# Exponentials and an index row in PSUM, fewer candidate additions, later weight reductions and a fixed order of the last products, in a decoder block on one core

## The chip, the cores and the metric

The kernel runs on one core of a Trainium2 chip. A core has a matrix engine (TensorE, PE in the profile, with PEld for its weight loads), a vector engine (VectorE, DVE), an activation engine (ScalarE, ACT), a general engine (GpSimd, POOL) and SyncE (SP), whose queue issues most DMAs. Each engine works through its own list of instructions in order and waits on semaphores for the others. Matmul results land in PSUM (8 banks of 128 x 512 fp32 here), everything else lies in SBUF. The metric is the device time of one execution in microseconds.

## What is computed

A decoder block over 512 tokens of 1024 channels: block-sparse attention and an RWKV-7 time mix run side by side, are merged by gates, and a product-key expert layer (PEER) follows. The parts that matter here, cut from the reference:

```python
mod = (jax.nn.silu(c) @ w_ada[l] + b_ada[l])[:, None, :]
sh1, sc1, gt1, sh2, sc2, gt2 = jnp.split(mod, 6, axis=-1)
...
qm = rope_partial(rms_norm(qm.reshape(B, S, MOBA_HEADS, HEAD_DIM), q_norm_g[l]), positions)
km = rope_partial(rms_norm(km.reshape(B, S, MOBA_HEADS, HEAD_DIM), k_norm_g[l]), positions)
...
w = -jax.nn.softplus(-(w0 + jnp.tanh(zw) @ w2)) - 0.5
decay = jnp.exp(-jnp.exp(w.astype(f32)))
...
top_s, top_i = lax.top_k(s, PEER_TOPK)
cand_s = (top_s[:, :, 0, :, None] + top_s[:, :, 1, None, :]).reshape(T, PEER_HEADS, PEER_TOPK * PEER_TOPK)
cand_i = (top_i[:, :, 0, :, None] * PEER_NKEYS + top_i[:, :, 1, None, :]).reshape(T, PEER_HEADS, PEER_TOPK * PEER_TOPK)
best_s, best_j = lax.top_k(cand_s, PEER_TOPK)
idx = jnp.take_along_axis(cand_i, best_j, axis=-1)
```

The expert layer then computes, for 384 of the tokens, gelu(x U) times a gate matrix times V over all 16384 experts in 128 blocks, and for the first 128 tokens it gathers the chosen rows of U and V one by one.

## The kernel before

The program is one list of operations; a scheduler that simulates the engines sets the order on each engine, by the priority of an operation (the order in the text, or a high-priority section), and by pacing hints (`follow`) that put one instruction behind another of the same engine without a wait. All matrix products of fp32 are made as three products of rounded halves (hi and lo).

The stages in order of time, with the lines of the profile:

- To about 98 us: the adaLN vector, the first norm, and the first columns of the input projection.
- 98 to 211 us: `rwkv_in`. For each of four groups of 128 channels (p = 0 to 3) `decays` (L481) makes e2 and e3, the falling and the growing exponentials of the summed decays (both 128 x 516, in SBUF, L494 and L495), and `elementwise` (L509) multiplies with them: KK (POOL, L515), the new kk (L517, L518), Kq (L525), RR (POOL, L527). Results go to DRAM. Meanwhile PE works on the queries and keys (`w_tm`, L452), and `qk_part` (L566) normalises each half of a result: sum of squares (L573), an inverse root by Newton steps (L161 to L166, eleven small DVE operations on 128 x 8), gain and rotation on POOL (L578 to L588), the product (L589) and four transposes on PE (L594).
- `inverses(0)` and `tokens(0)` (L387 on PE) start inside this stage; the inverse of chunk 0 solves its 16 x 16 blocks by thirty dependent small DVE operations (L661, L662; tile Yd).
- 211 to 560 us: the RWKV chunks, at high priority, with the attention (`scores`, `outputs`) and the gate projections (`gates`, `w_cm`, L422) as filling on PE; how much filling stands between two steps of the chain is set by `fill`.
- Through all this, `mods` computes the other four adaLN vectors in 32 steps. One step is a DMA of 512 KB of w_ada (wmod, three buffers, L175) and a multiply with a sum along the row on DVE (L176). Every `w_cm` and every second half of a `w_tm` calls one step.
- 560 to 700 us: projections, merge and second norm; 700 to 805 us: `queries`, which takes the top 16 of each score row on DVE.
- About 806 to 1030 us: `best`, for four tiles of 128 tokens. `best_of` (L1001) sums the candidates (nine additions of scores on DVE and nine of indices on POOL: L1017 eight times, L1019 once), takes the top 16 and finds their expert index: a comparison with the row 0 to 49 (`iota`, in SBUF, L1026), a product (L1027, on DVE for tile 1 and on POOL for the others) and a sum (L1029), 64 times each.
- From 875 us: 96 steps of `gates_dense`, each a one-hot pair (L1221 compares with a copy of `iota` that lies in PSUM, tile `iop`; L1225 on DVE or L1230 and L1231 on ACT) and four matmuls (L1238), with the dense products x U between them (`dense_h`, L1178; POOL or DVE make the lo half, L1172).
- To about 2014 us: `dense_v` and `products` (L1305) for each of 128 blocks; six PSUM accumulators, two for each 128 tokens t. At the end the accumulators are scaled, added and stored (L1335 to L1337).

Of the kernel before, what the change touches and what calls it, by code (L numbers as in the profile page):

```python
# [63 lines left out]
def kernel(ctx: ExitStack, tc: tile.TileContext, A):  # L64
# [501 lines left out]
    def qk_part(ps, hf, qi, g):  # L566
        qf = ahalf("qn")
        qn = qf.rearrange("p (h j) -> p h j", h=8)
        ACT.copy(qf, ps)
        sq = ahalf("qsq").rearrange("p (h j) -> p h j", h=8)  # L570
        ACT.activation(sq, qn, AF.Square)
        ss = sm.tile([128, 8], F32, name="qss")
        DVE.tensor_reduce(ss, sq, axis=AX.X, op=ALU.add)  # L573
# [11 lines left out]
        POOL.tensor_tensor(r1, x[:, :, :, 0:16], table(0, 0), op=ALU.mult)
        for a in (0, 8):
            POOL.tensor_tensor(r2[:, :, :, a:a + 8], x[:, :, :, 8 - a:16 - a], table(1, a), op=ALU.mult)
        POOL.tensor_tensor(x[:, :, :, 0:16], r1, r2, op=ALU.add)  # L588
        DVE.tensor_tensor(qn, qn, bc3(y, 64), op=ALU.mult)  # L589
        pT = attile()  # L590
        for c in range(2):
# [821 lines left out]
```

## Time and profile before

| | |
|---|---|
| median of 3 runs (range) | 2023.93 us (2022.27 to 2029.1) |
| the profiled execution | 2025.54 us |
| its span, first to last instruction | 2023.8 us |
| PE busy | 1915.9 us (95%) |
| DVE busy | 1510.3 us (75%) |
| ACT, POOL busy | 828.3 us, 775.6 us |
| mean granted clock of TensorE | 0.979 |

Busy shares are means over stages with different limits, so the rows below go by stage: windows give busy time of each engine and the granted clock of a stretch, waits say who waited for whom, and the timeline lists instructions with start and duration. An instruction that is held up inside its engine shows as a long duration, not as idle time.

### The profile page before, as it was taken

The numbers are of one execution on the slowest core, as the hardware profiler recorded it, in microseconds if no ns is written. First come the engines' busy times: TensorE is split into PE (matmuls) and PEld (weight loads), VectorE is DVE, ScalarE is ACT, GpSimd is POOL, SyncE is SP. The second block draws the span as 40 slices with busy tenths as digits, with TensorE's granted clock in tenths as the row PEclk, the third lists the DMA queues.
The fourth block names the chain that finished last, engine by engine and source line by source line (L and its number), as shares of the span: only waits on it lengthen the run. The fifth ranks groups of instructions, "written<-read, shape, count | busy, mean of one in ns | idle before, by whom it ended". The sixth has DMA issues, their size and how long they took to land.

```text
span 2023.8 us, 29453 instructions
## 1 busy us (share of the span) xinstructions
PE 1915.9 (95%) x10509; PEld 1669.0 (82%) x10509; DVE 1510.3 (75%) x3268; ACT 828.3 (41%) x1367; POOL 775.6 (38%) x631
## 2 busy tenths in 40 slices
PE   7987899999989899888999999999999999999997
PEld 5666777787868888877899998888899999999985
DVE  7798665546445578999977876888756788888885
ACT  5443233323313433356777763333333333333332
POOL 5555210010105322566656663222212444544551
PEclk9998899999989899999999999999999999999999
DMA  8664233321446423435568989999967999999893
GB/s 288 211 202 134 81 115 98 102 93 49 156 138 195 127 80 97 131 110 165 180 199 278 322 303 388 356 354 346 333 219 245 337 335 351 326 351 331 306 346 131
DMA packets 204326, 450.79 MB, mean 223 GB/s; under 512 B 16649, under 2 KB 105225, under 8 KB 204178
## 3 DMA queue, kind: packets, MB, share of 16 engines
q1 hardware_dynamic: 167024, 314.54, 46.1%
q0 software_dynamic: 36864, 134.23, 18.3%
q8 instruction: 83, 1.36, 0.3%
q14 instruction: 65, 0.53, 0.1%
q10 hardware_dynamic: 290, 0.13, 0.0%
HBM read 393.13 MB, written 55.71 MB: 222 GB/s over the span
## 4 chain that ended last, share of the span: by engine, by line
PE 69%; DVE 17%; DMA 4%; issue 2%; ACT 1%; POOL 0%; POOLq 0%; SPq 0%; DVEq 0%; ACTq 0%
PE acc L1305 23%; PE mm L1178 17%; PE mm L422 10%; PE rwp L387 8%; PE mm L452 4%; DMA vf<-in_peer_v 2%; PE pg L1238 2%; DVE ohg L1225 2%; DVE eq L1026 2%; DVE oh L1221 1%; DVE idf L1029 1%; DVE row L1143 1%; PE atp L868 1%; PE atp L842 1%; PE atp L994 1%
## 5 line engine op out<-in xcount | busy, mean ns | idle before, releaser
L1178 PE MATMUL mm<-x,whi 128*128 128x384 f32 x2048 | 542.2, 345 | 1.7 <-ACT ge L1183 1.7
L1178 PEld LDWEIGHTS mm<-x,whi 128*128 128x128 f32 x2048 | 372.7, 190 | 5.6 <-ACT ge L1183 2.0
L1178 PE MATMUL mm<-x,wlo 128*128 128x384 f32 x1024 | 350.8, 343 | 9.5 <-POOL wlo L1172 9.5
L1171 ACT CAST whi<-wf 128x1024 fp32r<-128x1024 f32 x128 | 134.7, 1052 | 290.8 <-PE mm L1178 223.7
L1305 PE MATMUL acc<-vl,ah 128*128 128x512 f32 x768 | 237.6, 390 | 2.7 <-DVE vl L1296 2.7
L1305 PE MATMUL acc<-vh,al 128*128 128x512 f32 x768 | 237.2, 390 | 0.0
L412 POOL TENSOR_TENSOR wlo<-wf,whi 128x1024 fp32r<-128x1024 f32 x33 | 80.9, 2450 | 399.2 <-ACT whi L409 309.9
L1305 PE MATMUL acc<-vh,ah 128*128 128x512 f32 x768 | 206.7, 390 | 3.3 <-ACT vh L1295 3.2
L1178 PEld LDWEIGHTS mm<-x,wlo 128*128 128x128 f32 x1024 | 194.6, 190 | 11.1 <-POOL wlo L1172 10.9
L1172 POOL TENSOR_TENSOR wlo<-wf,whi 128x1024 fp32r<-128x1024 f32 x66 | 163.5, 2479 | 102.4 <-ACT whi L1171 102.3
L1120 POOL DMA_INDIRECT row<-in_peer_u,gidx x96 | 113.2, 1179 | 233.2 <-DVE gh L1143 223.0
L1120 POOL DMA_INDIRECT row<-in_peer_v,gidx x86 | 124.1, 1443 | 154.1 <-DVE gacc L1150 142.5
L1296 DVE TENSOR_TENSOR vl<-vf,vh 128x1024 fp32r<-128x1024 f32 x128 | 157.5, 1231 | 22.5 <-ACT vh L1295 21.9
L1305 PEld LDWEIGHTS acc<-vh,ah 128*128 128x128 f32 x768 | 143.7, 188 | 34.5 <-ACT vh L1295 5.2
L1305 PEld LDWEIGHTS acc<-vl,ah 128*128 128x128 f32 x768 | 143.6, 188 | 31.0 <-DVE vl L1296 3.5
L1305 PEld LDWEIGHTS acc<-vh,al 128*128 128x128 f32 x768 | 144.1, 188 | 30.0
L1295 ACT CAST vh<-vf 128x1024 fp32r<-128x1024 f32 x128 | 134.7, 1054 | 17.2 <-DMA vf<-in_peer_v 17.2
L422 PE MATMUL mm<-X,whi 128*128 128x512 f32 x400 | 135.7, 411 | 3.3 <-ACT z L472 3.3
L1172 DVE TENSOR_TENSOR wlo<-wf,whi 128x1024 fp32r<-128x1024 f32 x62 | 75.9, 1224 | 84.1 <-ACT whi L1171 83.9
L1238 PE MATMUL pg<-ohg,oh 128*128 128x128 f32 x768 | 117.3, 287 | 22.0 <-ACT ohg L1231 15.2
L1143 DVE CUSTOM_DVE_ANT_0 row<-row,xtok 128x1024 f32<-128x1024 f32 x96 | 131.7, 1380 | 4.4 <-DMA row<-in_peer_u,gidx 4.4
L1238 PEld LDWEIGHTS pg<-ohg,oh 128*128 128x128 f32 x768 | 108.0, 192 | 31.6 <-ACT ohg L1231 19.0
(1195 smaller groups left out, 3807.5 us busy)
## 6 DMA issues: line engine op xcount, KB each, us to landing
wf<-in_peer_ut SPq DMA_DIRECT2D x128, 512.0 KB, 4.9
vf<-in_peer_v SPq DMA_DIRECT2D x128, 512.0 KB, 6.0
wmod<-in_w_ada SPq DMA_DIRECT2D x48, 512.0 KB, 4.3
G_d<-stg SPq DMA_DIRECT2D x12, 2048.0 KB, 9.4
wf<-in_w_in_c SPq DMA_DIRECT2D x30, 512.0 KB, 3.9
ge_d<-ge SPq DMA_DIRECT2D x50, 192.0 KB, 2.5
ger<-ge_d SPq DMA_DIRECT2D x50, 192.0 KB, 6.3
wf<-in_peer_wq SPq DMA_DIRECT2D x16, 512.0 KB, 3.5
```

The costliest lines, as they stand in the source:

```text
L387: i = f(*a, **k)
L422: i = fill(PE.matmul(ps, l[:, ks], r(k), start=k == 0 and n == 0, stop=k == nk - 1 and n == 2), 512)
L452: i = fill(PE.matmul(ps[:, c0:c0 + 256], l(4 * kh + k)[:, ts], r[:, cs], start=kh == 0 and tt % 2 == 0 and k == 0 and n == 0, stop=kh == 1 ...
L1120: i = POOL.indirect_dma_start(out=row, out_offset=None, in_=A[key], in_offset=bass.IndirectOffsetOnAxis(ap=gidx[:, s_:s_ + 1], axis=0))
L1143: DVE.tensor_tensor_reduce(out=row, in0=row, in1=xtok, op0=ALU.mult, op1=ALU.add, scale=1.0, scalar=0.0, accum_out=gh[:, s_:s_ + 1])
L1171: ACT.copy(uh, f)
L1172: (POOL if e < LAG else DVE).tensor_tensor(ul, f, uh.bitcast(F32), op=ALU.subtract)
L1178: i = PE.matmul(ps[:, 0:NTD], l[:, ks], r[:, k, 128:512], start=n == 0, stop=n == 23)
L1238: i = PE.matmul(pg[:, t * 128:(t + 1) * 128], oh2[:, t], ohg[:, t], start=True, stop=True)
L1295: ACT.copy(vh, f)
L1296: DVE.tensor_tensor(vl, f, vh.bitcast(F32), op=ALU.subtract)
L1305: i = PE.matmul(acc[2 * t + d], l[:, ts], r[:, d * 512:(d + 1) * 512], start=e == 0 and l is ah and r is vh, stop=e == 127 and l is al)
```

## The change

Six parts, all in one diff:

1. The growing exponentials e3 are written by ACT to a PSUM bank (`rwtile`) instead of SBUF, without their first column; that column and the last of e2 go to `ee` by two small ACT operations instead of two DVE copies.
2. A second copy of `iota` is put in PSUM (`ioe`) before `queries`, and the comparison of `best_of` reads it there.
3. The candidates are summed in six additions instead of nine: rows of equal length are taken together, with one candidate more (NCAND 51).
4. `qk_part` for one half becomes `qk_parts` for both: one Newton iteration on 128 x 16 in place of two on 128 x 8; the transposes are issued later, in the middle of the next `w_tm`, behind given matmuls (`marks`).
5. The 32 steps of `mods` are called by a variable number: none in `rwkv_in` and for queries and keys, one for the values and the first gates, two from the second gates on.
6. For the last two blocks of `products`, the matmuls of one t follow those of the t before.

```diff
-        mods(1, i)
+        mods(nmod[0], i)
...
             if tt == 3:
-                mods(1, i)
+                mods(nmod[0], i)
+            marks.append(i)
...
-        e2, e3 = half4_("e2"), half4_("e3")
+        e2, e3 = half4_("e2"), v4(rwtile())
         ACT.activation(e2, sg, AF.Exp, scale=-0.5 * KAPPA)
-        ACT.activation(e3, sg, AF.Exp, scale=0.5 * KAPPA)
-        DVE.tensor_copy(ee[:, :, 0, p], e3[:, :, 0])
-        DVE.tensor_copy(ee[:, :, 1, p], e2[:, :, 128])
+        ACT.activation(e3, sg[:, :, 1:], AF.Exp, scale=0.5 * KAPPA)
+        ACT.activation(ee[:, :, 0, p], sg[:, :, 0], AF.Exp, scale=0.5 * KAPPA)
+        ACT.activation(ee[:, :, 1, p], sg[:, :, 128], AF.Exp, scale=-0.5 * KAPPA)
...
-        DVE.scalar_tensor_tensor(v4(kk), v4(kk), 0.5, e3[:, :, 1:], op0=ALU.mult, op1=ALU.mult)
+        DVE.scalar_tensor_tensor(v4(kk), v4(kk), 0.5, e3, op0=ALU.mult, op1=ALU.mult)
...
-        DVE.tensor_tensor(v4(zk), v4(zk), e3[:, :, 1:], op=ALU.mult)
+        DVE.tensor_tensor(v4(zk), v4(zk), e3, op=ALU.mult)
...
+    def qk_parts(pss, qi, g):
+
+        ss, y, t = [sm.tile([128, 2, 8], F32, name=n) for n in ("qss", "qy", "qt")]
...
         newton(ss, y, t)
...
+        def channels_first(after):
+            for hf, qf in enumerate(qfs):
+                pT = attile()
+                for c in range(2):
+                    for i in range(2):
+                        o = (2 * c + i) * 128
+                        m = PE.transpose(pT[:, o:o + 128], qf[:, i * 256 + c * 128:i * 256 + (c + 1) * 128], ident)
+                        follow(m, after[hf])
...
                 pss = w_tm(A["w_in_t"][2 * qi + g], X)
-                for hf in range(2):
-                    qk_part(pss[hf], hf, qi, g)
+                if later:
+                    later.pop()(marks[2:4])
+                later.append(qk_parts(pss, qi, g))
...
-            for r1 in range(8):
-                n = 16 // (r1 + 1)
-                eng.tensor_tensor(dst[:, :, off:off + n], src[:, :, 0, r1:r1 + 1].broadcast_to([128, 4, n]), src[:, :, 1, 0:n], op=ALU.add)
-                off += n
+            for r1, m, n in ((0, 1, 16), (1, 1, 8), (2, 1, 5), (3, 2, 4), (5, 3, 2)):
...
-            DVE.tensor_tensor(eq, bc3(bf_[:, h_, k_:k_ + 8], NCAND), bcm(iota[:, 0:NCAND], 8), op=ALU.is_equal)
+            DVE.tensor_tensor(eq, bc3(bf_[:, h_, k_:k_ + 8], NCAND), bcm(ioe[0][:, 0:NCAND], 8), op=ALU.is_equal)
...
     attend(0)
+    nmod[0] = 2
     gates(range(G0, G1))
...
+    ioe.append(attile())
+    ACT.copy(ioe[0][:, 0:128], iota)
+    queries(first_q)
...
                         i = PE.matmul(acc[2 * t + d], l[:, ts], r[:, d * 512:(d + 1) * 512],
                                       start=e == 0 and l is ah and r is vh, stop=e == 127 and l is al)
+                        if len(es) > 1:
+                            follow(i, last)
```

The order that the scheduler makes of it, at three places. First DVE, in the middle of the thirty dependent steps of chunk 0's block inverse (tiles tm and Yd); L176 is a step of `mods`, qss, qy and qt belong to the norms of queries and keys. Before:

```order
L662 TENSOR_TENSOR Yd<-Yd,tm 128x8x8
L176 ISA wmod,modc<-wmod,scr 128x1024
L176 ISA modc 128x1
L661 TENSOR_TENSOR tm<-R,Yd 128x8x7
L573 TENSOR_REDUCE qss<-qsq 128x8
L662 TENSOR_TENSOR Yd<-Yd,tm 128x8x7
L574 TENSOR_SCALAR qss<-qss 128x8
L661 TENSOR_TENSOR tm<-R,Yd 128x8x6
L161 TENSOR_SCALAR qy<-qss 128x8
L662 TENSOR_TENSOR Yd<-Yd,tm 128x8x6
L162 TENSOR_SCALAR qy<-qy 128x8
```

and the same steps now:

```order
L681 TENSOR_TENSOR Yd<-Yd,tm 128x8x8
L680 TENSOR_TENSOR tm<-R,Yd 128x8x7
L681 TENSOR_TENSOR Yd<-Yd,tm 128x8x7
L680 TENSOR_TENSOR tm<-R,Yd 128x8x6
L681 TENSOR_TENSOR Yd<-Yd,tm 128x8x6
L680 TENSOR_TENSOR tm<-R,Yd 128x8x5
L681 TENSOR_TENSOR Yd<-Yd,tm 128x8x5
L680 TENSOR_TENSOR tm<-R,Yd 128x8x4
L579 TENSOR_REDUCE qss<-qsq 128x8
L681 TENSOR_TENSOR Yd<-Yd,tm 128x8x4
```

The reductions and almost all norm operations have left the chain. Between the first kk of p = 0 and the end of this chain, 9 steps of `mods` stood on DVE before, and none stands there now.

Second DVE, in the chunk steps between 260 and 560 us, where the steps of `mods` now stand (XX and XT are steps of chunk 1's inverse, rc and P belong to the attention's softmax):

```order
L864 ISA mx 128x1
L176 ISA wmod,modc<-wmod,scr 128x1024
L176 ISA modc 128x1
L176 ISA wmod,modc<-wmod,scr 128x1024
L176 ISA modc 128x1
L870 RECIPROCAL rc<-se 128x1
L710 TENSOR_TENSOR XX<-XX,rwp 128x512
L715 TENSOR_TENSOR XT<-XT,rwp 128x512
```

Most of them come in pairs; between the end of chunk 0's block inverse and the end of the last one there are 28 steps of `mods` now, and there were 17.

Third PE, the end of the program. Before, block 127's products of the rounding remainders (vl and al) end with all six accumulators:

```order
L1305 MATMUL acc2_11818<-vl_18381,ah_18374 128x512
L1305 MATMUL acc3_11819<-vl_18381,ah_18374 128x512
L1305 MATMUL acc2_11818<-vh_18380,al_18375 128x512
L1305 MATMUL acc3_11819<-vh_18380,al_18375 128x512
L1305 MATMUL acc4_11820<-vl_18381,ah_18374 128x512
L1305 MATMUL acc5_11821<-vl_18381,ah_18374 128x512
L1305 MATMUL acc4_11820<-vh_18380,al_18375 128x512
L1305 MATMUL acc5_11821<-vh_18380,al_18375 128x512
```

Now (vh_18263 is of block 126, vh_18274 of block 127):

```order
L1335 MATMUL acc3_11713<-vh_18274,al_18269 128x512
L1335 MATMUL acc4_11714<-vh_18263,ah_18257 128x512
L1335 MATMUL acc5_11715<-vh_18263,ah_18257 128x512
L1335 MATMUL acc4_11714<-vl_18264,ah_18257 128x512
L1335 MATMUL acc5_11715<-vl_18264,ah_18257 128x512
L1335 MATMUL acc4_11714<-vh_18263,al_18258 128x512
L1335 MATMUL acc5_11715<-vh_18263,al_18258 128x512
L1335 MATMUL acc4_11714<-vh_18274,ah_18268 128x512
L1335 MATMUL acc5_11715<-vh_18274,ah_18268 128x512
L1335 MATMUL acc4_11714<-vl_18275,ah_18268 128x512
L1335 MATMUL acc5_11715<-vl_18275,ah_18268 128x512
```

The last twelve matmuls all go to the accumulators 4 and 5, so 0 to 3 are complete twelve matmuls before the end.

## Rows read from the trace of the kernel before

**Rows 1.** From the page: busy time of each engine in us, with the share of the span and the count of instructions.

```profile
PE 1915.9 (95%) x10509; PEld 1669.0 (82%) x10509; DVE 1510.3 (75%) x3268; ACT 828.3 (41%) x1367; POOL 775.6 (38%) x631
```

**Rows 2.** Windows: for stretches of the span (start:end, length), busy us and count of PE, PEld, DVE, ACT and POOL, then the granted TensorE clock (1.00 is 2.4 GHz, 0.5 is 1.2 GHz), DMA share, GB/s.

```profile
97.70:154.20 56.50, 50.48 (x246) 36.13 (x247) 50.09 (x78) 23.31 (x36) 29.21 (x26) 0.97 0.64 205
154.20:188.60 34.40, 23.59 (x135) 19.23 (x134) 32.75 (x83) 13.25 (x24) 20.72 (x23) 0.80 0.50 166
188.60:211.30 22.70, 14.47 (x112) 13.19 (x110) 19.65 (x60) 6.38 (x10) 9.01 (x11) 0.90 0.28 85
...
260.00:560.00 300.00, 296.08 (x1890) 234.72 (x1890) 165.38 (x424) 95.62 (x220) 30.02 (x16) 1.00 0.33 104
...
700.00:800.00 100.00, 100.00 (x527) 85.24 (x526) 74.02 (x461) 31.87 (x50) 21.55 (x21) 1.00 0.24 78
800.00:870.00 70.00, 58.89 (x326) 57.21 (x324) 66.02 (x287) 24.57 (x35) 44.15 (x43) 0.95 0.41 128
870.00:1000.00 130.00, 113.51 (x665) 106.95 (x665) 130.00 (x404) 84.92 (x137) 83.78 (x90) 0.96 0.47 146
1000.00:1060.00 60.00, 57.81 (x366) 56.78 (x367) 47.52 (x109) 45.83 (x79) 32.27 (x19) 0.97 0.64 199
...
1300.00:1970.00 670.00, 670.00 (x3276) 597.74 (x3275) 535.91 (x658) 239.65 (x324) 253.50 (x203) 1.00 0.90 322
```

**Rows 3.** Waits of PE over the whole span: what waited for what, us in total, times, longest.

```profile
PE pg L1238 <- ACT ohg L1231: 15.2, 12, 2.8
PE mm L1178 <- POOL wlo L1172: 9.5, 3, 5.5
PE atp L594 <- DVE qn L589: 8.3, 1, 8.3
PE rwp L387 <- DVE Dk L645: 7.5, 3, 4.5
```

**Rows 4.** Timeline of DVE, 855 to 880 us: start us, duration us, engine, line, operation, tiles, shapes. L1026 reads two SBUF operands, L1221 one in SBUF and one in PSUM (atp).

```profile
872.23 2.47 DVE L1026 TENSOR_TENSOR eq<-wa,iota 128x400 f32<-128x400 f32 x1
...
876.50 0.68 DVE L1221 TENSOR_TENSOR oh<-sT,atp 128x512 f32<-128x512 f32 x1
```

**Rows 5.** Timeline of POOL in the same stretch; L1172 reads two SBUF operands.

```profile
871.54 2.73 POOL L1172 TENSOR_TENSOR wlo<-wf,whi 128x1024 fp32r<-128x1024 f32 x1
...
876.40 2.37 POOL L1172 TENSOR_TENSOR wlo<-wf,whi 128x1024 fp32r<-128x1024 f32 x1
```

**Rows 6.** Five lines of DVE, each from the view of that line: count, duration in ns (least/median/most), first and last start. L645 reads SBUF alone, without POOL beside it.

```profile
L1026 DVE TENSOR_TENSOR eq<-wa,iota x64: 522/566/2701, 822.1 to 1027.6; 128x400 f32<-128x400 f32 x64
...
L1221 DVE TENSOR_TENSOR oh<-sT,atp x96: 664/678/690, 874.6 to 1197.7; 128x512 f32<-128x512 f32 x96
...
L518 DVE SCALAR_TENSOR_TENSOR kk<-kk,e x4: 694/1970/2774, 101.8 to 158.0; 128x512 f32<-128x512 f32 x4
...
L525 DVE TENSOR_TENSOR zk<-zk,e x4: 819/1673/2819, 107.7 to 164.5; 128x512 f32<-128x512 f32 x4
...
L645 DVE TENSOR_TENSOR Dk<-C,dl x16: 678/689/698, 173.9 to 486.3; 128x512 f32<-128x512 f32 x16
```

**Rows 7.** The step of `mods` (L176) alone, over the three stretches 97.7 to 211.3 us: DVE busy us.

```profile
sum 113.60, DVE 12.01; mean DVE 4.00
```

**Rows 8.** Groups of instructions by line over the whole span: count, busy us, mean ns, idle before. L165 and L166 are two of the Newton steps of the query and key norms.

```profile
L518 DVE SCALAR_TENSOR_TENSOR kk<-kk,e 128x512 f32<-128x512 f32 x4 | 7.4, 1852 | 0.1
...
L525 DVE TENSOR_TENSOR zk<-zk,e 128x512 f32<-128x512 f32 x4 | 7.0, 1746 | 0.0
...
L165 DVE SCALAR_TENSOR_TENSOR qt<-qt,qss 128x8 f32<-128x8 f32 x24 | 5.1, 211 | 0.3
...
L166 DVE SCALAR_TENSOR_TENSOR qy<-qt,qy 128x8 f32<-128x8 f32 x24 | 5.0, 211 | 0.3
```

**Rows 9.** Timeline of DVE, chunk 0's block inverse: its start, two of its steps and a step of `mods` between them, its end.

```profile
188.62 0.22 DVE L658 COPY Yd<-dl 128x128 f32<-128x128 f32 x1
...
198.15 2.31 DVE L662 TENSOR_TENSOR Yd<-Yd,tm 128x72 f32<-128x72 f32 x1
...
200.90 1.22 DVE L176 CUSTOM_DVE_ANT_0 wmod<-wmod,scr 128x1024 f32<-128x1024 f32 x1
...
210.50 0.17 DVE L662 TENSOR_TENSOR Yd<-Yd,tm 128x8 f32<-128x8 f32 x1
```

**Rows 10.** Groups of DVE by line in 800 to 1060 us.

```profile
L1026 DVE TENSOR_TENSOR eq<-wa,iota 128x400 f32<-128x400 f32 x64 | 54.6, 880 | 0.0
...
L1017 DVE TENSOR_TENSOR wb<-vi 128x8 f32<-128x8 f32 (+5 forms) x56 | 11.8, 267 | 0.0
```

**Rows 11.** Timeline of the end, all engines: block 126's first products on PE, block 127's vl on DVE, the last products, and the scaling and the last addition of the outputs.

```profile
2005.44 1.52 PE L1305 MATMUL acc<-vh,ah 128*128 128x512 f32 x6
...
2006.73 1.23 DVE L1296 TENSOR_TENSOR vl<-vf,vh 128x1024 fp32r<-128x1024 f32 x1 [0.43 <-ACT vh L1295]
...
2011.76 1.29 DVE L1335 TENSOR_TENSOR o<-acc,gt 128x512 f32<-128x512 f32 x2 [3.81 <-PE acc L1305]
...
2013.15 0.61 PE L1305 MATMUL acc<-vh,al 128*128 128x512 f32 x2
...
2018.02 1.26 POOL L1336 TENSOR_TENSOR o<-o,hh 128x512 f32<-128x512 f32 x1 [1.83 <-DVE o L1335]
```

More of the change, by code (lines that the diff above doesn't have):

```diff
@@ L29 @@
 NWF = 3
-NCAND = 50
+NCAND = 51
 LAG = 66
@@ L398 @@
     nsplit = [0]
+    nmod, marks = [0], []
     def wload(src):
@@ L564 @@
     qT, kT, vtok = {}, {}, {}
[L566 to L573, printed above, removed]
+    def qk_parts(pss, qi, g):
+        ss, y, t = [sm.tile([128, 2, 8], F32, name=n) for n in ("qss", "qy", "qt")]
+        qfs = []
+        for hf in range(2):
+            qf = ahalf("qn")
+            ACT.copy(qf, pss[hf])
+            sq = ahalf("qsq").rearrange("p (h j) -> p h j", h=8)
+            ACT.activation(sq, qf.rearrange("p (h j) -> p h j", h=8), AF.Square)
+            DVE.tensor_reduce(ss[:, hf], sq, axis=AX.X, op=ALU.add)
+            qfs.append(qf)
@@ L585, in qk_part @@
[L585 to L591, printed above, removed]
-            for i in range(2):
-                o = (2 * c + i) * 128
-                PE.transpose(pT[:, o:o + 128], qf[:, i * 256 + c * 128:i * 256 + (c + 1) * 128], ident)
@@ L595, in qk_part, with table @@
-        dst = kvhalf("qkT")
-        ACT.copy(dst, pT)
-        for c in range(2):
-            (qT, kT)[qi][hf, 2 * g + c] = v2(dst)[:, c]
+        for hf, qf in enumerate(qfs):
+            qn = qf.rearrange("p (h j) -> p h j", h=8)
+            POOL.tensor_tensor(qn, qn, qkg[:, qi:qi + 1].broadcast_to([128, 8, 64]), op=ALU.mult)
+            r1, r2 = [at.tile([128, 2, 4, 16], F32, name=nm, bufs=1) for nm in ("r1", "r2")]
+            x = qf.rearrange("p (i h j) -> p i h j", i=2, h=4)
+            def table(n, a):
+                return sincos[:, 2 * hf:2 * hf + 2, n:n + 1, a:a + 8 if n else 16].broadcast_to([128, 2, 4, 8 if n else 16])
+            POOL.tensor_tensor(r1, x[:, :, :, 0:16], table(0, 0), op=ALU.mult)
+            for a in (0, 8):
+                POOL.tensor_tensor(r2[:, :, :, a:a + 8], x[:, :, :, 8 - a:16 - a], table(1, a), op=ALU.mult)
+            POOL.tensor_tensor(x[:, :, :, 0:16], r1, r2, op=ALU.add)
+            DVE.tensor_tensor(qn, qn, bc3(y[:, hf], 64), op=ALU.mult)
@@ new lines, in channels_first @@
+        def channels_first(after):
+            for hf, qf in enumerate(qfs):
+                pT = attile()
[4 more added lines that the diff above has]
+                        follow(m, after[hf])
+                dst = kvhalf("qkT")
+                ACT.copy(dst, pT)
+                for c in range(2):
+                    (qT, kT)[qi][hf, 2 * g + c] = v2(dst)[:, c]
@@ L600, in qkv @@
+        return channels_first
     def qkv():
+        later = []
         for qi in (1, 0):
@@ L608, in qkv @@
         for g in range(2):
+            nmod[0] = 1
             pss = w_tm(A["w_in_t"][4 + g], X)
+            if later:
+                later.pop()(marks[2:4])
             for tt in range(4):
@@ L884 @@
     hd_ = [dr.tile([128, 4, 2, 256], F32, name=f"h_d{i}") for i in range(2)]
-    vals, inds = {}, {}
+    vals, inds, ioe = {}, {}, []
     def top16(src, v, ix):
@@ L1299, in products @@
     def products(es, parts):
+        i = None
         for t in range(3):
-            ts = slice(t * 128, (t + 1) * 128)
+            ts, last = slice(t * 128, (t + 1) * 128), i
             for e, (ah, al, vh, vl) in zip(es, parts):
```

17 lines of the change are left out of this document (9 added, 8 removed).

## Prediction

> **What bounds the kernel now.** I read the page first: PE is busy for 95% of the span and DVE for 75% [rows 1]. Then the windows [rows 2], where the two bounds part. From 1300 to 1970 us PE is busy for all 670 us at a clock of 1.00, and from 260 to 560 us for 296 of 300 us: there only PE's own work counts, and the change takes none away. Two stretches are different. From 97.7 to 211.3 us PE is busy for 50.5 + 23.6 + 14.5 = 88.5 of 113.6 us, and its granted clock is 0.97, 0.80 and 0.90; DVE is busy for 50.1 + 32.8 + 19.7 = 102.5 us. From 800 to 1060 us PE is busy for 230.2 of 260 us at 0.95 to 0.97, and DVE for 243.5, without a gap from 870 to 1000 us. The waits of PE [rows 3] name DVE directly (qn, Dk), or ACT and POOL, which in these stretches work on what DVE or the same SBUF operands give them. So DVE sets the pace in both, and what a busy DVE does there must be seen next.
>
> The timeline shows it [rows 4, 5]. The comparison L1026 starts at 872.23 and takes 2.47 us; POOL's L1172 runs from 871.54 to 874.27, and the comparison ends just behind it. L1221, a larger comparison that reads its index row from PSUM, starts at 876.50 inside another L1172 (876.40 to 878.77) and takes 0.68 us. Over all instances [rows 6] L1026 goes from 522 to 2701 ns with a median of 566, L1221 from 664 to 690. So a DVE operation with two SBUF operands stands still while POOL reads SBUF, and one with an operand in PSUM does not. L518 and L525, which read e3 from SBUF, show the same (694 to 2774 and 819 to 2819 ns).
>
> **The change part by part: 97.7 to 211.3 us.**
> Steps of `mods`: nine leave, 12.0 us of DVE [rows 7].
> e3 in PSUM: L518 and L525 take 7.4 + 7.0 = 14.4 us for eight operations [rows 8]; at 0.69 us, the time of L645 and the least of L518 [rows 6], they take 5.5, so 8.9 less.
> Newton steps: one call of eleven operations and a scaling goes for every two. Six of the eight calls stand before the end of chunk 0's inverse, so 3 x 12 = 36 operations of 0.21 us [rows 8] leave, 7.6 us by their durations; as neighbours overlap in DVE's pipeline I count 6.
> The two copies to `ee` I count at nothing: on DVE they are small, and on ACT, busy for 23.3 of 56.5 us in the first of the three windows [rows 2], the small exponentials lie beside other work. If that cover fails, four pairs of them delay the tanh behind them; eight at no more than the 0.69 us of a 512-wide operation would be about 5 us.
> Together 27 us of DVE. How much of it is on the path? The least is the wait of 8.3 us for qn [rows 3]: PE stood before the transposes until the block inverse on DVE was through, and both the transposes (now behind matmuls of the next `w_tm`, with qn finished before the inverse starts) and the chain have been freed. The inverse runs from 188.62 to 210.67, 22 us for thirty small operations, with a step of `mods` of 1.22 us and a stall of 2.31 us among them [rows 9]; most of what stood between them is gone, and the stalls behind POOL stay. The most is all 27 us: PE has 25.1 us idle, and 0.03 x 56.5 + 0.20 x 34.4 + 0.10 x 22.7, doubled, is 21.7 us at 1.2 GHz, in which matmuls take twice as long. PE still has to wait for data that go through DRAM and for ACT, so I take two thirds, 18 us, between the ends 8 and 27.
>
> **800 to 1060 us.**
> The 64 comparisons take 54.6 us [rows 10]; at the median of 566 ns they take 36.2, so 18.4 less. Reading PSUM costs nothing more by L1221 (678 ns for 512 elements) against L645 (689 ns for as many in SBUF) [rows 6].
> [...]
> Additions: 24 fewer on DVE, at no more than L1017's mean of 0.27 us [rows 10] 6.5 us, and at half of that, as they overlap, 3. NCAND 51 adds 2% to 64 comparisons, products and sums, about 2 us by the 566 ns, of which most products lie on POOL; I count 1 on DVE.
> So 20 us less for DVE. PE has 29.8 us idle there and about 2 x (0.05 x 70 + 0.04 x 130 + 0.03 x 60) = 21 us at 1.2 GHz [rows 2], so there is room for it. But products of tile 1 (L1027 on DVE) and the additions still read two SBUF operands and will stand behind POOL where they come next, and PE waits for ACT's one-hot rows too (15.2 us [rows 3]). I take three quarters, 15 us; the ends are 6 and 20.
> The bank that `ioe` takes leaves two instead of three for scores in `queries`. PE is busy for all of 700 to 800 us [rows 2], which hides it: I count nothing. Uncovered it is at most a copy's time for each of 16 score banks, 16 x 0.69 = 11 us by an operation of 512 elements.
>
> **260 to 560 us, and the end.**
> The 32 steps of `mods` move here and behind: 28 instead of 17 between the first and the last block inverse, mostly in pairs, ahead of steps of the chain such as XX, and queued in front of them. Eleven more at 1.22 us [rows 9] are 13.4 us of DVE, which is busy for 165 of 300 us [rows 2], and each chain step has filling on PE beside it. With 17 steps all idle time of PE is 3.9 us; in proportion 28 would make it 6.4. I take 2 us of loss, between -1 (the DMAs of w_ada leave the early stage) and 13. On SP's queue the wmod loads are now in pairs ahead of weights and chunk loads; the DMA share there is 0.33, which hides them.
> The end: before, PE's last product ends at 2013.76 and POOL's last addition at 2019.28, 5.5 us later, because all six accumulators come free together [rows 11]. Now only two outputs are left: two scalings (1.29 us as in the row) and POOL's addition (1.26) end 2.7 us after the last product. The new order makes block 127's vl (ready at 2007.96) needed after 8 of its matmuls, at 2005.44 + 8 x 0.25 = 2007.44 (1.52 us for six, as in the row), so PE waits 0.5 us. The gain is 5.5 - 2.7 - 0.5, about 2 us; the ends are 0 and 3.
>
> The sum: 18 + 15 + 2 - 2 = 33 us. The profiled execution took 2025.54 us for a span of 2023.8, 1.7 us around it, and the median of the runs is 1.6 us below it. So the span becomes about 1991, and from the median 2023.93 - 33, rounded, 1991 us. The bounds together give gains from 8 + 6 + 0 - 13 = 1, to 27 + 20 + 3 + 1 = 51 us.
>
> **Rivals.**
> The stall moves on. POOL runs as before, and the next DVE operation with two SBUF operands (L517, L521, the additions, L1027) waits where e3 or L1026 waited. For it speaks that L1026, L1027 and L1017 come in a row; against it, that after 870 us L1027 is POOL's own and most of DVE's neighbours of L1026 are L1221, L1225 and L1029, which read at most one operand from SBUF. Then half of 8.9 and of 18.4 is left, 13.7 less, and with the shares on the path the gain is about 33 - 10, and if PE's chains through ACT also hold, 15: 2009 us.
> PE gains its clock as well. If the gaps close, the 21.7 + 21 us at 1.2 GHz shrink too, PE does its work sooner, and the whole bound is reached: 51 us, near 1975. Against it: DVE then is still as long as PE in both stretches.
> The time does not change: the DVE time falls away but PE waits for ACT and DRAM in the same places, and the early gain is lost before 560 us. For it speaks only that ACT stands first among PE's waits. 2021 us.
> Slower: the pairs of `mods` decide. XX, XT and the masks of a chunk stand behind two steps of 1.22 us; PE idles for it if the filling between two chain steps is shorter than that. From about 15 exposed pairs, 15 x 2.44 = 37 us, the loss passes the gain: 2024 + 4 = 2028. Against it: PE idle in that stretch is 3.9 us with 17 steps there.
>
> **How the numbers follow.** The forecast, gains of 24 to 42 us: 0.57, its own range 1982 to 2000. The stall moves on, 8 to 24 us: 0.24. With the clock, more than 42 us: 0.11. No change: 0.04. Slower: 0.04. 0.3% of the time is 6 us, about what a measurement of this kernel can tell from no change. So faster 0.92, same 0.04, slower 0.04. The range from 1974 to 2010 holds the first three cases but for the weakest gains, and leaves out about 0.15.
>
> **What would show it.** L1050 (the comparison now) near 0.57 us throughout, with no instance over 0.7; L522 and L529 at 0.7. PE idle below 12 us in the stretch that ended at 211.3, with chunk 0's block inverse in 12 to 14 us, and the granted clock above 0.92 there. DVE no longer without a gap in the 130 us behind the first one-hot. In the chunk stage, PE idle under 8 us. POOL's last addition less than 3.5 us after the last product. I am wrong if the comparisons from PSUM still stretch to 2 us, if other two-operand lines (L1017's successors, L521) lengthen by what these lose, or if PE's waits in the chunk stage reach 15 us.

## The result, and the profile after

The changed kernel takes 2005.51 us (median of 5 runs, 2004.14 to 2009.46) against 2022.27 for the kernel before beside it: a ratio of 0.9915, with a 95% interval from 0.9902 to 0.9927. That is 17 us less; the forecast was 33. The profiled execution took 2006.55 us for a span of 2004.8.

The page, against [rows 1]: DVE has 33 us less to do, PE 4.

```profile
PE 1912.2 (95%) x10509; PEld 1669.4 (83%) x10509; DVE 1477.2 (74%) x3188; ACT 827.6 (41%) x1376; POOL 758.7 (38%) x607
```

Windows over the same stretches as [rows 2], with the same columns (the program is some 10 us further on in them):

```profile
97.70:154.20 56.50, 53.98 (x295) 40.51 (x294) 44.23 (x70) 29.70 (x51) 32.40 (x33) 1.00 0.52 168
154.20:188.60 34.40, 25.53 (x148) 20.94 (x147) 27.39 (x62) 8.60 (x15) 11.12 (x17) 0.80 0.29 92
188.60:211.30 22.70, 19.42 (x133) 18.13 (x131) 17.34 (x39) 5.41 (x9) 9.13 (x11) 0.85 0.14 47
...
260.00:560.00 300.00, 295.44 (x1849) 234.89 (x1847) 180.73 (x444) 92.39 (x209) 32.22 (x16) 0.98 0.41 132
...
800.00:870.00 70.00, 60.17 (x315) 58.05 (x314) 69.13 (x277) 22.97 (x33) 39.94 (x36) 0.93 0.41 131
870.00:1000.00 130.00, 118.48 (x739) 113.89 (x738) 127.66 (x416) 97.83 (x165) 90.49 (x86) 0.99 0.55 170
1000.00:1060.00 60.00, 60.00 (x401) 60.00 (x400) 35.60 (x91) 47.65 (x81) 26.69 (x14) 1.00 0.63 193
1060.00:1200.00 140.00, 133.69 (x847) 130.94 (x845) 107.11 (x210) 93.79 (x157) 92.07 (x52) 0.99 0.92 314
```

PE's idle time fell from 25 to 14.7 us in the first three rows, and from 16.5 to 11.5 in 870 to 1000. In 1000 to 1060 PE has no gap while DVE has 35.6 of 60 us: there DVE is no longer what PE waits for.

The lines of DVE that the change was to shorten, against [rows 6] (least/median/most in ns), and the products L1051 that follow the comparison in tile 1:

```profile
L1050 DVE TENSOR_TENSOR eq<-wa,atp x64: 549/567/573, 813.6 to 995.3; 128x408 f32<-128x408 f32 x64
...
L522 DVE SCALAR_TENSOR_TENSOR kk<-kk,rwp x4: 679/688/690, 98.4 to 148.6; 128x512 f32<-128x512 f32 x4
...
L529 DVE TENSOR_TENSOR zk<-zk,rwp x4: 675/676/680, 103.5 to 152.9; 128x512 f32<-128x512 f32 x4
...
L1051 DVE TENSOR_TENSOR eq<-eq,wb x16: 555/572/2750, 815.3 to 849.5; 128x408 f32<-128x408 f32 x16
```

None of the first three stretches any more; L1051, with two operands in SBUF, still does.

So where did half of the gain go? The starts of six instructions (us, from the view of each line) cut the program into pieces. They stand here for all kernels of this study; the columns are the last chunk's state products SBD (L819), the last step of the last block inverse (P, L705), the second norm on PE (L436), the last comparison (L1050), the first product into the accumulators (L1335) and the span:

| kernel | SBD | P | second norm | last comparison | first product | span |
|---|---|---|---|---|---|---|
| before | 504.4 | 543.3 | 690.8 | 1027.6 | 1222.6 | 2023.8 |
| changed | 487.1 | 537.8 | 682.3 | 995.3 | 1206.6 | 2004.8 |
| e1, steps of mods as before | 497.0 | 535.9 | 682.6 | 995.3 | 1204.1 | 2005.3 |
| e2, before + steps of mods | 494.3 | 543.4 | 687.8 | 1023.4 | 1219.8 | 2020.8 |
| e3, changed, gate_rows late | 491.9 | 531.7 | 676.1 | 989.7 | 1197.1 | 1997.9 |
| e4, changed, pairs sooner | 499.8 | 541.8 | 686.2 | 998.7 | 1207.0 | 2006.3 |
| e5, changed, iota in SBUF | 489.8 | 540.5 | 685.5 | 1010.6 | 1216.1 | 2015.3 |
| e6, changed, e3 in SBUF | 489.8 | 539.0 | 682.9 | 995.6 | 1202.9 | 2001.9 |
| e7, changed, nine additions | 487.6 | 538.2 | 683.5 | 1006.3 | 1203.6 | 2003.1 |
| e8, changed, no order at the end | 487.1 | 534.6 | 681.6 | 994.7 | 1202.7 | 2003.9 |
| e9, before + qk_parts | 500.8 | 539.7 | 685.8 | 1022.4 | 1218.9 | 2021.6 |
| e10, changed, transposes at once | 488.2 | 537.3 | 680.1 | 993.1 | 1201.0 | 2000.0 |
| e11, before, gate_rows late | 509.7 | 546.6 | 690.5 | 1026.4 | 1222.2 | 2023.3 |
| e12, before + iota in PSUM | 502.9 | 541.8 | 693.2 | 1014.2 | 1210.8 | 2010.0 |

At the second norm e5 differs from the changed kernel by 3.2 us and e12 from the kernel before by 2.4, though nothing is edited ahead of it: differences of 3 us there say nothing.

In the changed kernel the gain is 17.3 us at SBD, 5.5 at P, 8.5 at the second norm, 32.3 at the last comparison and 16.0 at the first product. A start alone does not say how much work PE has done by then. PE's windows from the beginning to SBD and to the second norm (stretch, length, busy us (count), granted clock, DMA share, GB/s), before and then changed:

```profile
0.00:504.40 504.40, 463.44 (x2712) 0.97 0.42 137
...
0.00:690.80 690.80, 633.85 (x3785) 0.96 0.45 146
```

```profile
0.00:487.10 487.10, 454.39 (x2686) 0.96 0.43 141
...
0.00:682.30 682.30, 631.79 (x3784) 0.96 0.45 148
```

At SBD the changed kernel has made 26 matmuls fewer, all of them of the late attention, which takes 5.4 us between SBD and P there against 1.0 before: some 4 us of the 17.3 are work put off and not time won. At the second norm the counts agree, and the 8.5 us are 6.4 of PE's idle time (56.9 to 50.5) and 2.1 of its busy time. The first P of chunk 0 is a fair mark too (851 and 856 matmuls): it starts at 221.9 before and at 207.3 now, a gain of 14.6. For the same matmuls up to the second norm PE is busy for 625.8 us (e1) to 634.6 (e11) over the 14 profiles, so one profile alone can be several us off there.

So the gain shrinks twice: from 14.6 to 8.5 between the first P and the second norm, and behind the last comparison. The theory for the first: the pace of `mods` changes PE's order around the last chunk's inverse. For the second: PE is full again (60 of 60 us), so time of DVE beyond that is worth nothing.

### The profile page after: what moved, and what is told of

Same layout as the page of the kernel before. It is cut to its first block, busy times and chain, and to the rows that moved or that the text cites. A ratio compares the mean times of both kernels' runs of the same rounds, so it can differ in the third digit from the quotient of the medians.

```text
span 2004.8 us, 29360 instructions
## 1 busy us (share of the span) xinstructions
PE 1912.2 (95%) x10509; PEld 1669.4 (83%) x10509; DVE 1477.2 (74%) x3188; ACT 827.6 (41%) x1376; POOL 758.7 (38%) x607
## 4 chain that ended last, share of the span: by engine, by line
PE 78%; DVE 14%; DMA 3%; ACT 2%; issue 2%; POOL 1%; SPq 0%; POOLq 0%; DVEq 0%; ACTq 0%
PE acc L1335 25%; PE mm L1203 19%; PE mm L423 12%; PE rwp L387 8%; PE mm L454 5%; PE pg L1263 3%; DVE ohg L1250 2%; DVE oh L1246 1%; DVE eq L1050 1%; PE atp L861 1%; PE atp L887 1%; DVE idf L1053 1%; DVE row L1168 1%; DMA vf<-in_peer_v 1%; DVE eq L1051 1%
## 5 line engine op out<-in xcount | busy, mean ns | idle before, releaser
L1203 PE MATMUL mm<-x,whi 128*128 128x384 f32 x2048 | 543.3, 346 | 1.2 <-ACT ge L1208 1.2
L1335 PE MATMUL acc<-vl,ah 128*128 128x512 f32 x768 | 237.7, 390 | 2.4 <-DVE vl L1324 2.4
L1335 PE MATMUL acc<-vh,al 128*128 128x512 f32 x768 | 237.6, 390 | 0.0
L413 POOL TENSOR_TENSOR wlo<-wf,whi 128x1024 fp32r<-128x1024 f32 x33 | 80.1, 2428 | 391.7 <-ACT whi L410 375.0
L1335 PE MATMUL acc<-vh,ah 128*128 128x512 f32 x768 | 207.1, 390 | 2.2 <-ACT vh L1323 2.2
L1335 PEld LDWEIGHTS acc<-vh,ah 128*128 128x128 f32 x768 | 143.9, 188 | 32.8 <-ACT vh L1323 3.2
L1335 PEld LDWEIGHTS acc<-vl,ah 128*128 128x128 f32 x768 | 143.5, 188 | 31.5 <-DVE vl L1324 3.7
L1335 PEld LDWEIGHTS acc<-vh,al 128*128 128x128 f32 x768 | 144.1, 188 | 30.0
L423 PE MATMUL mm<-X,whi 128*128 128x512 f32 x400 | 137.3, 414 | 2.5 <-ACT z L475 2.5
L1263 PE MATMUL pg<-ohg,oh 128*128 128x128 f32 x768 | 112.7, 281 | 17.1 <-ACT ohg L1256 9.1
L1269 ACT COPY stg<-pg 128x512 f32<-128x512 f32 x96 | 105.6, 1115 | 48.8 <-PE pg L1263 48.7
```

The lines of the kernel that those rows point to most:

```text
L423: i = fill(PE.matmul(ps, l[:, ks], r(k), start=k == 0 and n == 0, stop=k == nk - 1 and n == 2), 512)
L1203: i = PE.matmul(ps[:, 0:NTD], l[:, ks], r[:, k, 128:512], start=n == 0, stop=n == 23)
L1263: i = PE.matmul(pg[:, t * 128:(t + 1) * 128], oh2[:, t], ohg[:, t], start=True, stop=True)
L1269: ACT.copy(stg[:, :, t4 * 4:t4 * 4 + 4].rearrange("p i t -> p t i"), pg.rearrange("p (t i) -> p t i", t=4))
L1335: i = PE.matmul(acc[2 * t + d], l[:, ts], r[:, d * 512:(d + 1) * 512], start=e == 0 and l is ah and r is vh, stop=e == 127 and l is al)
```

## Experiments

**The pace of mods, undone and alone (e1, e2).** e1:

```diff
-    nmod, marks = [0], []
+    nmod, marks = [1], []
...
-    nmod[0] = 2
+    nmod[0] = 1
```

> The changed kernel with the steps of mods called one at a time from the first w_tm on, as before; all else of the change stays. The changed kernel's gain over the kernel before stands at 17 us when the SBD products of the last chunk start (497.6 to 479.8), and at 8.5 us at the second norm (690.8 to 682.3): some 9 us are lost between 487 and 540. Theory A (the pace of mods sets where gate_rows, attention and filling stand in PE's order around the last chunk's chain; with it undone PE's order there is that of the kernel before): the early gain shrinks from 17 to about 9, for nine steps of 1.22 us are back on DVE before 211 us, two thirds of their 12 us on the path, but nothing is lost after 487; the gain at the second norm is 8 to 10 and the time 2003 to 2008. Rival B (what is lost after 487 is lost whatever the order is, because the chain of the last chunk waits for something else): the gain at the second norm is 0 to 2 and the time 2011 to 2015. Rival C (the steps of mods cost nothing early, as DVE was relieved by e3 and the Newton steps): the gain is 17 at SBD, 17 at the second norm, the time 1995 to 1999.

e2 puts the same numbers (0, 1, 2) into the kernel before:

> The kernel before with only the steps of mods moved, as in the change: none up to the keys and queries, one for the values and the first gates, two from then on. Theory A: 7 to 9 us gained by 260 us (nine steps of 1.22 us fewer on DVE, two thirds of it on the path) and 8 to 10 lost between 487 and 560; the time is 2020 to 2026, no change. Rival B (the loss after 487 comes from other parts of the change): the gain is kept, 2013 to 2017. Rival D (the pairs on DVE delay the chain in all chunks): slower, 2028 or more.

Measured: e1 2007.54 us, ratio to before 0.9932 (0.9915 to 0.9948); e2 2020.32, 0.9992 (0.9980 to 1.0005). Both are in theory A's range; B, C and D fall. In PE's list of instructions around the last chunk, e1 reads as the kernel before and e2 as the changed one. The windows of PE, of the matmuls of the RWKV chain alone (L387), over the 16 us behind the last SBD operation, show what that does. Columns: stretch, length, busy us (count), granted clock, DMA share, GB/s. First the changed kernel, then e1:

```profile
487.60:503.60 16.00, 2.95 (x18) 1.00 0.50 155
```

```profile
497.40:513.40 16.00, 6.03 (x42) 1.00 0.55 169
```

18 matmuls of the chain instead of 42. The groups of PE in the first 12.4 us of that stretch in the changed kernel say what stood there instead (line, tiles, count, busy us):

```profile
L378 PE MATMUL mm<-dg,ones 128*128 128x128 f32 x22 | 4.0, 294 | 0.3 <-DVE dg L377 0.3
L423 PE MATMUL mm<-X,whi 128*128 128x512 f32 x11 | 3.6, 404 | 0.0
L887 PE MATMUL atp<-PT,vtok 128*64 128x128 f32 x22 | 3.0, 280 | 0.0
...
L387 PE MATMUL rwp<-ident,XT 128*128 128x128 f32 x4 | 0.6, 272 | 0.0
```

These are `gate_rows` (L378), gate projections (L423) and late attention (L887). PE is busy for 12.1 of these 12.4 us, so no wait shows it. From SBD to P it takes 50.7 us in the changed kernel and 49.1 in e2, but 38.9 in the kernel before and in e1. PE's windows of that whole stretch say what is new in it, with the same columns: first `gate_rows`, before and changed, then the gate projections (L422 before, L423 now).

```profile
504.40:543.30 38.90, 4.18 (x24) 1.00 0.41 128
```

```profile
487.10:537.80 50.70, 4.39 (x24) 0.93 0.44 141
```

```profile
504.40:543.30 38.90, 19.42 (x77) 1.00 0.41 128
```

```profile
487.10:537.80 50.70, 24.90 (x92) 0.93 0.44 141
```

`gate_rows` is not new there. New are 15 matmuls of the gate projections and 26 of the late attention (34 against 8), and the granted clock was 0.93 instead of 1.00: e8, with the same groups in the stretch at a clock of 1.00, takes 47.5 us.

What the moved steps give early (e2: 9.1 us at the first P) has shrunk to 3.0 by the second norm, and the whole part is worth 1.6 us (0.9992 of 2023) to 3.4 us (0.9932 less 0.9915), which the runs hardly tell from nothing. Nor do the other early parts bring anything that shows without it: e1 has the ratio of the comparison alone (0.9932, and 0.9934 in e12 below). Up to the second norm PE is idle for 56.8 us in e1 and 57.4 in e2, as before (56.9), and for 47.8 to 54.1 in the eight kernels that have both (the changed one, e3 to e8, e10).

**gate_rows behind the last gates, in both kernels (e3, e11), and the pairs sooner (e4).**

```diff
-    gate_rows(2, 5)
     gates(range(12, 16))
+    gate_rows(2, 5)
```

> The changed kernel with gate_rows(2, 5) called behind the last four gates instead of ahead of them, so that its 32 matmuls and what waits for the last sums of mods leave the place around 466 to 503 us. Theory A1 (gate_rows and the wait for the sums of mods behind it hold up the last chunk's chain on PE): most of the 9 us come back, 1996 to 2000. Theory A2 (it is the late attention and the two blocks of 20 and 25 filling matmuls in front of the chain): 2003 to 2007, as the changed kernel. Rival D (gate_rows then stands in front of the projections and is waited for): slower than 2007.

> The kernel before with gate_rows(2, 5) behind the last four gates. In the kernel before the chain takes 38.5 us from the last SBD to the last step of the last inverse, as short as in the changed kernel with gate_rows late (39.5), and 50.2 in the changed kernel. Theory A1 (gate_rows at its place costs only with the new pace of mods): 2019 to 2025, no change. Rival G (gate_rows between the steps of the last inverse is better filling whatever the pace is): 2013 to 2018.

e4 sets `nmod[0] = 2`, not 1, for the values:

> The changed kernel with two steps of mods a call from the values on, not only from the second gates on: the 32 steps are done 10 calls sooner (26 steps at two, instead of one, end before the last gates), gate_rows does not wait for them, and attention stands ahead of the last chunk's chain less often. Theory A: part or all of the 9 us lost after 487 comes back, 1996 to 2002. Theory A2 with the filling in front of the chain as the cause: here 19 and 23 filling matmuls still stand in one piece in PE's order there, so 2003 to 2007. Rival D (pairs of 1.22 us on DVE cost in the chunks): slower, 2008 or more.

e3: 1998.60 us, 0.9882 (0.9862 to 0.9902), faster than the kernel before; against the changed kernel (0.9915, from 0.9902) the intervals touch. The time is in theory A1's range, and SBD to P is 39.8 us: 16 of the 24 matmuls of `gate_rows` and 16 of the gate projections have left the stretch, while the 34 of the late attention are still in it. So moving `gate_rows` undoes the delay; that it was the cause is not shown, as it stood there before, too. The timeline of PE there shows four matmuls of `gate_rows` at a time between dependent steps of the last inverse, with the filling now where the chain must wait anyway:

```profile
535.12 1.16 PE L387 MATMUL rwp<-XT,P 128*128 128x128 f32 x8
536.11 0.61 PE L378 MATMUL mm<-dg,ones 128*128 128x128 f32 x4
...
541.57 1.16 PE L387 MATMUL rwp<-RR,Bq 64*128 64x128 f32 x8
542.65 0.71 PE L378 MATMUL mm<-dg,ones 128*128 128x128 f32 x4
```

e11: 2020.88, 0.9976 (0.9961 to 0.9990): in the kernel before, where the chain already took 38.9 us, the same edit brings 5 us by the ratio and nothing by the second norm of the profile, whose own time was 2025.08 us. That is less than rival G wanted, and not clearly A1's nothing; e3 is 7 us by the ratios ahead of the changed kernel, so the times do not decide whether late `gate_rows` helps only with the new pace (A1) or with any (G). e4: 2005.89, 0.9918 (0.9901 to 0.9935): no gain, and in A2's range, though SBD to P is 42.0 us with no late attention in it. SBD is 12.7 us later than in the changed kernel, and PE has made 36 matmuls more by then (2722): the same work in another order.

**The comparison, undone and alone (e5, e12), and the additions (e7).** e5 (e12 is the reverse, in the kernel before, with `ioe`):

```diff
-            DVE.tensor_tensor(eq, bc3(bf_[:, h_, k_:k_ + 8], NCAND), bcm(ioe[0][:, 0:NCAND], 8), op=ALU.is_equal)
+            DVE.tensor_tensor(eq, bc3(bf_[:, h_, k_:k_ + 8], NCAND), bcm(iota[:, 0:NCAND], 8), op=ALU.is_equal)
```

> The changed kernel with one operand moved back: the comparison L1050 reads iota in SBUF again (the copy in PSUM is still made, and its bank stays taken). Theory L (a DVE operation with two SBUF operands stands still while POOL reads SBUF): the 64 comparisons stretch again, median near 570 ns, some over 2 us, sum near 54 us instead of 36; the last comparison comes some 20 us later (995.3 to about 1015), and as PE and the DMAs bound the stretch behind 1060, 7 to 10 us of it are left at the end: 2012 to 2016. Rival P (the gain in the middle comes from the additions or from the program being earlier): 2004 to 2008. Rival Q (PSUM alone is not what keeps the comparison short): no stretch, sum near 36 us, and 2004 to 2008.

> The kernel before with part 2 of the change alone: the comparison of best_of reads the index row from a PSUM bank. Theory L: the 64 comparisons at 0.57 us, 36 us in all instead of 54.6, the last one 10 to 15 us earlier against the second norm, and 7 to 11 us of it left at the end: 2012 to 2017. Rival P (it needs the six additions to be of use): 2018 to 2025.

> The changed kernel with the nine additions of scores and nine of indices and NCAND 50. My sum had 3 us of DVE for the additions and -1 for the 51st candidate, and three quarters of it on the path: 1 to 2 us slower than the changed kernel, 2005 to 2009. Rival P (the additions carry the gain of the middle): 2010 to 2014. Rival T (the 51st candidate costs as much): 2003 to 2006.

e5: 2017.08 us, 0.9966 (0.9955 to 0.9977); e12: 2011.00, 0.9934 (0.9914 to 0.9954); e7: 2005.01, 0.9911 (0.9894 to 0.9928). Theory L holds on both sides, 1 us outside its times in each (the 64 comparisons take 54.0 us in all in e5 and 34.4 in the changed kernel): alone this one operand is worth 13 us (1 - 0.9934 of 2023), and of the 17 us of the whole change 7 are left without it. The comparison in e5, and in e12:

```profile
L1050 DVE TENSOR_TENSOR eq<-wa,iota x64: 553/572/2765, 816.6 to 1010.6; 128x408 f32<-128x408 f32 x64
```

```profile
L1026 DVE TENSOR_TENSOR eq<-wa,atp x64: 514/557/571, 824.2 to 1014.2; 128x400 f32<-128x400 f32 x64
```

The additions cannot be told from nothing: 2005.01 lies in the range of the sum (2005 to 2009) and in rival T's. In e7 the last comparison is 11.0 us later than in the changed kernel, yet the first product 3.0 us earlier. From the second norm to the first product the kernels with the comparison in PSUM take 517.6 (e12) to 524.3 us (the changed kernel's profile; seven others 520 to 522), those with it in SBUF 530.6 (e5) to 533.1 (e9): some 11 us (14 in e12). Behind the last comparison, up to 1060 us, PE has no gap, and more time of DVE, as from the additions, buys nothing.

**The early parts: e3 (e6), qk_parts (e9), the place of the transposes (e10).** e6:

```diff
-        e2, e3 = half4_("e2"), v4(rwtile())
+        e2, e3 = half4_("e2"), half4_("e3")[:, :, 1:]
```

> The changed kernel with e3 back in SBUF, still without its first column and with the two small exponentials on ACT. Theory L: L522 and L529 stretch again to a sum of 13 to 15 us for eight (5.5 now), two thirds of these 9 us are on the path to the first block inverse, which begins 5 to 7 us later; the chain keeps that up to the last chunk: 2009 to 2014. Rival R (what comes early is lost whole around the last chunk): the last step of the last inverse at the same time within 2 us, 2004 to 2008. Rival S (the exponentials in PSUM cost their readers more than the stall): faster, below 2003.

e9 is the kernel before with `qk_parts`, `marks` and `later` of the diff:

> The kernel before with part 4 of the change alone: one Newton iteration for both halves and the transposes in the middle of the next w_tm. With e3 back in SBUF nothing was lost (2004.4), and with the steps of mods back the second norm was still 8.2 us ahead of the kernel before. Theory Q (this part carries what is left of the early gain): the second norm 7 to 9 us ahead of the kernel before, and 2013 to 2018. Rival R (the transposes are late only because DVE is late, so without the relief by mods and e3 PE waits for the first block inverse as before): within 3 us of the kernel before, 2020 to 2026.

```diff
-                later.append(qk_parts(pss, qi, g))
+                qk_parts(pss, qi, g)(None)
...
-                        follow(m, after[hf])
+                        if after:
+                            follow(m, after[hf])
```

> The changed kernel with the four transposes of each half issued at once, behind their product, as before; the merged Newton iteration stays. Theory Q1 (the wait of 8.3 us for qn in front of the transposes was the loss): PE waits for qn again, the second norm 5 to 8 us later, 2010 to 2014. Theory Q2 (the fewer operations on DVE carry it): 2003 to 2008.

e6: 2004.38 us, 0.9904 (0.9887 to 0.9922). L522 and L529 take 11.1 us for eight instead of 5.4 (13 to 15 expected), and the time is in rival R's range. Theory L fell for the time, not for the stall. R's reason does not hold either: little comes early that could be lost, for the first P of chunk 0 starts only 1.3 us later (208.6 against 207.3), less than in e5, where nothing is edited ahead of it (210.1). e9: 2023.53, 0.9995 (0.9980 to 1.0010), rival R's range. What PE waits for from 97 to 262 us in e9 (us, times, longest), beside [rows 3], gives a reason:

```profile
PE rwp L387 <- DVE Dk L662: 7.7, 2, 6.0
PE rwp L387 <- DVE XT L685: 7.3, 1, 7.3
PE mm L423 <- ACT z L475: 3.3, 1, 3.3
```

The wait of 8.3 us for qn is gone, and one of 7.3 us for XT, the result of the same block inverse, has come. e10: 2001.81, 0.9889 (0.9868 to 0.9910). Q1 falls: with the transposes at once PE has no wait for qn, and the time is no longer than the changed kernel's (3.7 us shorter by the medians, with intervals that overlap, so Q2, 1 us below its numbers). Where DVE has been relieved, the later place of the transposes is not needed.

By the start of the first P the parts add up: 221.9 before, 212.8 in e2 (9.1 us) and 217.5 in e9 (4.4), and 1.3 for e3, together 14.8; the changed kernel has 14.6. With 2.8 us between e5 and the changed kernel there, this fits better than it can be known. By the end e2 and e9 keep 1 to 2 us each.

**The order at the end, undone (e8).**

```diff
-                        if len(es) > 1:
-                            follow(i, last)
```

> The changed kernel without the order of the last two blocks' products. My sum gave 2 us: 2007 to 2009, with POOL's last addition 5.5 us after the last product. Rival (the order only moves the wait): 2005 to 2006, last addition 2.7 us after the last product and a wait of PE for vl, or 5.5 us with an earlier last product.

2005.48 us, 0.9911 (0.9895 to 0.9927): the rival's number, not told apart from the changed kernel's. The traces do: in e8 POOL's last addition ends 5.5 us after the last product (1993.86 to 1999.39). In the changed kernel it is 2.9 us, from 1997.41 to 2000.29, against [rows 11]:

```profile
1996.80 0.61 PE L1335 MATMUL acc<-vh,al 128*128 128x512 f32 x2
1997.28 1.29 DVE L1367 TENSOR_TENSOR o<-acc,gt 128x512 f32<-128x512 f32 x2 [0.89 <-issue]
1998.49 0.68 DVE L1368 TENSOR_TENSOR o<-o,hh 128x512 f32<-128x512 f32 x1
1998.65 1.64 POOL L1368 TENSOR_TENSOR o<-o,hh 128x512 f32<-128x512 f32 x1 [1.11 <-DVE o L1367]
```

From the first product to the end of the span the changed kernel takes 798.2 us and e8 801.2. This stretch does not show the 3 us to be the order's: e1 and e3, whose last addition also ends 2.9 us after the last product, take 801.2 and 800.8.

## Why the prediction was right and wrong

The direction was right, and so was the mechanism for the lines that were changed: the comparison with both operands in SBUF takes up to 2765 ns (e5), and with one in PSUM at most 573 in the changed kernel; e3's two readers, against [rows 6], take at most 690 and 680. The size was not: 33 us against 17, by these terms.

**mods in 260 to 560 us, -2: the step that failed.** It was priced by PE's idle time, scaled with the count of steps, and for idle time that was near: 4.6 us in the 260 to 560 window against 3.9 [rows 2], and 2.6 more between the first P and the second norm (22.6 against 20.0). But the gain falls by 6.1 us between these two marks, from 14.6 to 8.5, and in e2 from 9.1 to 3.0, while in e1 it stays at 8.2. So by these profiles the term was -6. The rest sat in PE's busy time, which the price left out: with the new pace other filling stands in the last chunk's stretch, and the granted clock there was 0.93 against 1.00. The upper end of 13 covers it. The price looked at DVE's queue alone; what the pace does to PE's order was not followed. Which of the moved groups makes the delay, and why the clock was lower, stays open.

**97.7 to 211.3 us, 18.** 14.6 at the first P: about right, and then in part lost by the term above. Of its parts mods brought 9.1 (8 forecast, two thirds of 12), the Newton steps with the transposes 4.4 (4), e3 1.3 (6): two thirds on the path held for two of the three. The stall hardly moved on here: the two lines ahead of e3's readers, L521 and L525 (L517 and L521 before), take 9.2 us in all against 8.0, where e3's readers lose 9.0. The signs failed in part: PE idle 14.7 us instead of below 12, and the granted clock 1.00, 0.80 and 0.85 instead of above 0.92. The forecast reckoned with matmuls twice as long at half the clock: in the kernel before, two 128x512 matmuls on Dk (L387) took 2.07 us at a granted clock of 0.50 (at 174.66 us) and 1.10 at 1.00 (at 186.78), 1.9 times; the traces give the clock as a share of full speed, not in GHz. The block inverse takes 17.3 us (179.02 to 196.34) by the measure that gave 22, instead of 12 to 14. Both include a wait of some 2 us behind the first copy; the thirty steps alone took 19.6 us (191.11 to 210.67) and take 15.3 (181.01 to 196.34), since three of them still stand still. The timeline of DVE, against [rows 9]:

```profile
188.00 2.31 DVE L681 TENSOR_TENSOR Yd<-Yd,tm 128x64 f32<-128x64 f32 x1
...
191.09 1.18 DVE L681 TENSOR_TENSOR Yd<-Yd,tm 128x48 f32<-128x48 f32 x1
...
195.14 1.20 DVE L681 TENSOR_TENSOR Yd<-Yd,tm 128x8 f32<-128x8 f32 x1
```

The others take 0.17 to 0.28 us, but for one of 0.49. POOL works at 187.84 to 190.23 (L413), 190.87 to 192.21 and 195.04 to 196.30 (L585): each step ends with it, within 0.08 us. Not all of POOL's work holds such a step up: two of them (192.83 and 193.11) took 0.25 and 0.23 us beside L594 (192.70 to 193.30). So the stall is shown here for single lines, not for every operation with two operands in SBUF.

**800 to 1060 us, 15.** The lines behaved as forecast (0.567 us, none over 0.573; the forecast of no cost for PSUM held, too: 557 ns for 400 elements in e12, 566 before). By the path it was 11 us, 7.5 in the changed kernel's own profile. Three quarters was too much, because DVE stops being the bound at about 1000 us, and because in `best(1)` nothing came of it: from the first comparison to the first one-hot product it is 53.6 us before (822.1 to 875.7) and 53.8 after. There the rival "the stall moves on" was right. DVE's groups by line in this stretch of the changed kernel, 811 to 868 us (busy us, mean ns):

```profile
L1051 DVE TENSOR_TENSOR eq<-eq,wb 128x408 f32<-128x408 f32 x16 | 15.7, 1012 | 0.0
L1050 DVE TENSOR_TENSOR eq<-wa,atp 128x408 f32<-128x408 f32 x21 | 11.1, 564 | 0.0
...
L1224 DVE CAST ii<-idf 128x128 int32<-128x128 f32 x1 | 2.4, 2426 | 0.0
```

In the same stretch before, 819.3 to 876.3, these were 12.2 us for the products, 19.0 for the comparisons and 0.2 for the cast. So the comparisons lose 7.9 us, and the two lines that come next take 5.7 of them back.

**The end, 2.** 2.6 us by the last addition; held, though the medians do not show it.

8.5 us at the second norm, 7.5 from there to the first product (531.8 against 524.3) and 3.0 behind it (801.2 against 798.2) make up the 19.0 us between the profiled spans. That the result lies inside the range is in part luck, for it does so for another reason than the one given there: a case of half the gain was foreseen for the stall that moves on, which decided in `best(1)` alone, and not for the order of PE.

## What to carry to other kernels

A program whose order is fixed ahead can lose time where PE's waits do not show it (SBD to P, 38.9 to 50.7 us here): compare the start of the same instruction of the critical chain at several places, and count what the busy engine has done up to each of them, or work put off is read as time won. When a step of a shared side job is moved, look at what that does to the order on the other engines. Time taken from DVE counted here only up to the point where PE has no gap: of 32.3 us at the last comparison 16.0 were left at the first product. One operand of one line brought 13 us; the five other parts together bring 7 (e5), and none of them by itself can be told from nothing by its time.

## What the runs showed of the hardware that was not expected

A cast with a single SBUF operand also stood still behind POOL. The timeline of POOL and DVE in the changed kernel:

```profile
854.22 2.35 POOL L1197 TENSOR_TENSOR wlo<-wf,whi 128x1024 fp32r<-128x1024 f32 x1
854.23 2.43 DVE L1224 CAST ii<-idf 128x128 int32<-128x128 f32 x1
```

The cast starts 0.01 us behind POOL's subtraction and ends 0.09 us behind it: 2.43 us, where the shortest of the three casts of this line takes 209 ns. One operand in SBUF is thus no safe sign by itself; which line will be held next has to be read from the least and the greatest time of each line.
